# A hybrid decoder block: SBUF tiles of one size and one place, a weight chunk cut finer, a convolution's history kept apart

## The chip, the cores and the metric

The kernel runs on one core of one Trainium2 chip. A core has a matrix engine (PE; its weight loads are listed as PEld), a vector engine (DVE), an activation engine (ACT), a general engine (POOL), and a queue engine (SP) that issues every DMA of this kernel. The on-chip memory SBUF has 128 partitions; matmuls read their two operands from it and write to PSUM banks. The metric is the device time of one execution in microseconds (us), as a median over runs.

## What is computed

One decoder layer in float32 on a sequence of 2048 tokens and 1024 channels. Two groups of four heads (gated DeltaNet, and retention) share an input projection; their outputs are concatenated, projected and added to the input. Then follows a gated MLP with a causal convolution of width 3 over time between the up-projection and the activation.

```python
def _conv_glu_mlp(x, w_up, conv_w, w_down):
    hdn = jnp.einsum('bsd,df->bsf', x, w_up)
    hdn = _causal_dwconv(hdn, conv_w)
    g, u = jnp.split(hdn, 2, axis=-1)
    return jnp.einsum('bsf,fd->bsd', jax.nn.silu(g) * u, w_down)

def reference(x, ...):
    h = x
    for l in range(DEPTH):                      # DEPTH = 1
        n = _rms_norm(h, attn_norm_w[l])
        proj = jnp.einsum('bsd,dc->bsc', n, w_in[l])
        (gq, gk, gv, gg, ga, gb, rq, rk, rv, rg) = jnp.split(proj, split_idx, axis=-1)
        o_gdn = _gated_deltanet(gq, gk, gv, gg, ga, gb, ...)
        o_ret = _retention(rq, rk, rv, rg)
        mix = jnp.concatenate([o_gdn, o_ret], axis=-1)
        h = h + jnp.einsum('bsm,md->bsd', mix, w_out[l])
        n2 = _rms_norm(h, mlp_norm_w[l])
        h = h + _conv_glu_mlp(n2, w_up[l], mlp_conv_w[l], w_down[l])
    return _rms_norm(h, final_norm_w)
```

## The kernel before

**Precision.** Each operand of a large matmul is split into a rounded high part (an ACT copy) and a remainder (a DVE subtraction), stored as two halves of one tile. `mm3` (lines 91 to 97) multiplies high by high (line 95), high by low (96) and low by high (97), so that each product costs three matmuls.

**Three stages.** `mixers` (0 to 1364 us) makes the two head groups and the output projection, in four blocks of 512 tokens. `mlp_up` (1364 to 2306 us) makes the up-projection by a scheme of seven products (Strassen's), in two passes `q` over 22 groups of output channels; the convolution, the gating and the seven combinations for the next stage follow each group, and the combinations go to DRAM (`aud`). `mlp_down` (2330 to 2773 us) makes the down-projection in seven passes over eight token pairs.

**Tiles.** Every SBUF tile is made by `unit` with `U1` = 1056 floats (4,224 bytes) a partition, whatever it holds, so that any tile can take any other's place. A planner that runs at build time takes the count of buffers for each tag (the constants at the head and `BUFS`), gives each tile an address, puts the instructions of each engine in an order, and sets the waits. In the program before, tiles begin at 1,152 + 4,224 k bytes, k from 0 to 53; that is at 0, 128, 256 or 384 modulo 512.

**The order of the mixers.** `ORDER` names the items of a block in the order in which they are handed to the planner: `pro` (transposed input, its split `n1`, the row norms), `k0` (retention keys of the first head pair, and 8 extra columns `ab` from which `dec` makes the decays of the DeltaNet heads), `a0` to `a3` (a DeltaNet head: decay matrix `D`, keys and queries, values, and `gdn_base`, line 467 on, which writes the matrix `NA` to DRAM in transposed pieces, line 472, and solves a triangular system on POOL), `g0` to `g3` (its recurrence), `q`, `k`, `v`, `h` (retention), `G0` to `G3` (gates), `B0` to `B3` (output projection) and `Bn` (`n2`, line 711 on: the second norm, which scales four tiles `n2s` on DVE, line 724, and stores them). A name with a leading "-" stands for the same item of the block before. Weight chunks are loaded one item ahead (`LA` = 1).

**Weight chunks.** `load_chunk` (line 173 on) loads a chunk in pieces of `step` columns: in block 0 the raw weights (`wraw`, 2 buffers, line 185), which are split by ACT and DVE (187, 188) and stored split in DRAM (191); in later blocks the stored pieces (181). The chunk of `k0` has 264 columns for each of 8 row blocks; its pieces of 528 columns hold two row blocks each, in four tiles `wk`, and `wrow` finds row block k in tile k // 2.

**The convolution of the MLP.** `group` (line 832 on) collects the pre-activation of 1024 tokens in a tile `uc` of 2 + 1024 columns. In the second pass its first two columns are the last two of the first pass, kept in `mhalo` (line 873) and copied in by POOL (line 837). ACT makes tap 2 (867), DVE adds taps 1 and 0 (870), each over the shifted 1024 columns. `prep_x` (line 774 on) makes the split combinations of the input at the start of each pass, on POOL (786), ACT (767) and DVE (768).

Of the kernel before, what the change touches and what calls it, by code (L numbers as in the profile page):

```python
# [8 lines left out]
F32 = mybir.dt.float32  # L9
F32R = mybir.dt.float32r  # L10
AF = mybir.ActivationFunctionType
ALU = mybir.AluOpType
# [2 lines left out]

NW = 5
LA = 1
NHH = 3
NUU = 4
NVR = 5  # L20
NVV = 18
# [1 line left out]
NST = 4  # L23
NUC = 2
NACC = 6
NWU = 9
NWO = 5
NRAW = 2
BUFS = {"n1": 8, "ykq": 5, "kv": 6, "NA": 5, "TT": 2, "o": 4, "n2s": 4, "mT": 8, "xk": 2, "ca": 2, "h": 2,
        "mix": 4, "D": 4, "rk": 2, "rq": 2, "rv": 4, "Ar": 1, "Y": 2, "Nb": 2, "rot": 1, "rrow": 1}  # L30

ORDER = ("pro k0 dec a1 a0 q0 v0 h0 h1 a2 g1 q1 a3 g2 v1 G2 g0 k1 h2 g3 G0 h3 G1 G3 B0 B1 B2 B3 Bn")
P = 128
S = 2048
D = 1024
KT = D // P
TB = 512
# [4 lines left out]
NF = DFF // P  # L42
NP = NF // 2
# [3 lines left out]
ORD_DN = [1, 2, 6, 7, 5, 3, 4]  # L47


U1 = 1056  # L50


def unit(pool, tag, shape, dt=F32, **kw):

    n = int(np.prod(shape[1:]))
    t = pool.tile([P, U1], dt, tag=tag, name=tag, **kw)[:, :n]
    if len(shape) == 3:
        t = t.rearrange("p (a b) -> p a b", a=shape[1])
    elif len(shape) == 4:
        t = t.rearrange("p (a b c) -> p a b c", a=shape[1], b=shape[2])  # L60
    return t
# [3 lines left out]
def hybrid_block(ctx, tc, x, xT, w_kq, w_v, w_g, w_rk, w_r, w_o, w_u, w_d, cols, rows, fnr, masks, rot, out):  # L65
# [7 lines left out]
    NCOL = cols.shape[1]  # L73
    base = cp.tile([P, U1], F32, name="base")
    colt = base[:, :NCOL]
# [40 lines left out]
def mixers(ctx, tc, marks, drp, mm3, gamma, mhalf, n1w, n2w, gcw, gv127, epsr, n2d, hd,  # L116
           x, xT, w_kq, w_v, w_g, w_rk, w_r, w_o, rows, masks, rot):
    nc = tc.nc
    PE, ACT, DVE, POOL = nc.tensor, nc.scalar, nc.vector, nc.gpsimd
# [6 lines left out]

    pers, used = [], [U1]

    def pc(*shape):
        n = int(np.prod(shape))  # L130
        if used[0] + n > U1:
            pers.append(cp.tile([P, U1], F32, name=f"pers{len(pers)}"))
            used[0] = 0
# [33 lines left out]
        POOL.memset(t, 0.0)  # L167


    WQ = 528  # L170
    cache = {}

    def load_chunk(key, src):
        n = src.shape[1]
        step = WQ if n == 4 * WQ else 512
        qs = []
        for o in range(0, n, step):
            tg, nb = ("wco", NWO) if key[0] == "o" else ("wk", 4) if step == WQ else ("wc", NW)
            wc = unit(wp, tg, [P, 2, step], F32R, bufs=nb)
            if (key, o) in cache:  # L180
                nc.sync.dma_start(wc[:, :, :step].bitcast(F32), cache[key, o])
            else:
                if o % (2 * step) == 0:
                    raw2 = unit(wp, "wraw", [P, 2, step], bufs=NRAW)
                    nc.sync.dma_start(raw2.rearrange("p a n -> p (a n)"), src[:, o:o + 2 * step])
                raw = raw2[:, o // step % 2]
                ACT.activation(wc[:, 0], raw, AF.Copy)
                DVE.tensor_tensor(wc[:, 1], raw, wc[:, 0].bitcast(F32), op=ALU.subtract)  # L188
                nm = f"wd{len(cache)}"
                dt_ = cache[key, o] = drp.tile([P, 2, step], F32, name=nm, tag=nm, bufs=1)  # L190
                nc.sync.dma_start(dt_, wc[:, :, :step].bitcast(F32))
            qs.append(wc)
        return qs
# [4 lines left out]
        return t[:, 0, o:o + P], t[:, 1, o:o + P]  # L198

    def wrow(w, k, n):  # L200
        o = (k % 2) * n
        t = w[k // 2]
        return t[:, 0, o:o + n], t[:, 1, o:o + n]

    def al(tag, shape, dt=F32):
        return unit(ap_, tag, shape, dt, **({"bufs": BUFS[tag]} if tag in BUFS else {}))

# [37 lines left out]
    def A_items(b, st):  # L245
# [35 lines left out]
        def tokmajor(w, ncol, evac):  # L281
            n1 = st["n1"]
            for t in range(NT):
                ps = bank("tok")
                mm3(ps[:, :ncol],
                    [(n1[k][:, 0, t * P:(t + 1) * P], n1[k][:, 1, t * P:(t + 1) * P])
                     + wrow(w, k, ncol) for k in range(KT)])
                evac(t, ps)
# [445 lines left out]
    for b in range(NB + 1):  # L734
        for name in ORDER.split():
            c = b - 1 if name[0] == "-" else b
# [8 lines left out]
    for i, it in enumerate(seq):  # L745
        while nxt < len(order) and nxt <= done + la:
            loaded[order[nxt]] = load_chunk(*seq[order[nxt]][:2])
            nxt += 1
        if it[0] is not None:
            it[2](loaded.pop(i))  # L750
            done += 1
        else:
            it[2](None)
# [4 lines left out]
def mlp_up(ctx, tc, marks, drp, mm3, mcw, mhalo, n2d, wud, aud, w_u):  # L758
    nc = tc.nc
    PE, ACT, DVE, POOL = nc.tensor, nc.scalar, nc.vector, nc.gpsimd  # L760
    xp = ctx.enter_context(tc.tile_pool(name="xp", bufs=1))
    up = ctx.enter_context(tc.tile_pool(name="up", bufs=2))
    psu = ctx.enter_context(tc.tile_pool(name="psu", bufs=8, space=PSUM))
    T2 = 2 * TB
# [32 lines left out]
    def load_w(q, g):  # L797
        ws = {}

        def wtile(i):  # L800
            return unit(up, "wu", [P, 2, TB], F32R, bufs=NWU)
        if q == 1:
# [27 lines left out]
    def group(q, g, ws, xc, st):  # L830
        f0, kind = g // 2, g % 2
        us = []
        for j in range(2):
            u = unit(up, "uc", [P, 2 + T2], bufs=NUC)
            ci = kind * NF + f0 + j * NP
            if q:
                POOL.tensor_copy(u[:, :2], mhalo[:, ci])
            us.append(u)
        c11, c12 = us[0][:, 2:2 + TB], us[0][:, 2 + TB:]
        c21, c22 = us[1][:, 2:2 + TB], us[1][:, 2 + TB:]  # L840

        def prod(i, ps=None):
            first = ps is None
            if first:
                ps = psu.tile([P, TB], F32, tag="pp", name=f"p{i}")
            w = ws[i]
            mm3(ps, [(w[:, 0, kt * P:(kt + 1) * P], w[:, 1, kt * P:(kt + 1) * P], xc[i, kt][:, 0], xc[i, kt][:, 1])
                     for kt in range(4)], first=first, chk=not first)
            return ps
        add = lambda o, ps, a: DVE.tensor_tensor(o, ps, a, op=ALU.add)  # L850
        p1 = prod(1)
        ACT.activation(c12, p1, AF.Copy)
        prod(2, p1)
        ACT.activation(c11, p1, AF.Copy)
        add(c12, prod(6), c12)
        add(c21, prod(7), c12)
        p5 = prod(5)
        add(c22, p5, c21)
        add(c21, prod(4), c21)
        prod(3, p5)  # L860
        add(c12, p5, c12)
        accs = []
        for j in range(2):
            u = us[j]
            ci = kind * NF + f0 + j * NP
            acc = unit(up, "acc", [P, T2], bufs=NACC)
            ACT.activation(acc, u[:, 2:], AF.Copy, scale=mcw[:, ci, 2:3])  # L867
            for s in (1, 2):
                o = 0 if q else s
                DVE.scalar_tensor_tensor(acc[:, o:], u[:, 2 + o - s:2 - s + T2], mcw[:, ci, 2 - s:3 - s], acc[:, o:],  # L870
                                         op0=ALU.mult, op1=ALU.add)
            if q == 0:
                POOL.tensor_copy(mhalo[:, ci], u[:, T2:])
            accs.append(acc)
        if kind == 0:
            for a in accs:
                ACT.activation(a, a, AF.Silu)
            st["g"] = accs
            return
        for j in range(2):  # L880
            DVE.tensor_tensor(accs[j], st["g"][j], accs[j], op=ALU.mult)
        a11, a21 = accs[0][:, :TB], accs[0][:, TB:]
        a12, a22 = accs[1][:, :TB], accs[1][:, TB:]

        sts = [unit(up, "st", [P, 2, TB], bufs=NST) for j in range(2)]

        def comb(i, op, a, b_):
            t = sts[i // 2][:, i % 2]
            POOL.tensor_tensor(t, a, b_, op=op)
            return t  # L890
        s1 = comb(0, ALU.add, a21, a22)
        s2 = comb(1, ALU.subtract, s1, a11)
        s3 = comb(2, ALU.subtract, a11, a21)
        s4 = comb(3, ALU.subtract, a12, s2)
        for i, src in {1: a11, 2: a12, 4: a22, 5: s1, 6: s2, 7: s3, 3: s4}.items():
            marks["a", q, f0] = nc.sync.dma_start(aud[q, i][f0], src)
# [6 lines left out]
    for n, (q, g) in enumerate(gs):  # L903
        ws = nxt
        if n and g == 0:
            xc = prep_x(q)
        if n + 1 < len(gs):
            nxt = load_w(*gs[n + 1])
        group(q, g, ws, xc, st)
# [4 lines left out]
def mlp_down(ctx, tc, marks, mm3, sfa, mhalf, hd, aud, w_d, fnr, out):  # L914
# [77 lines left out]
    def addh(t, dh):  # L992
        h = unit(wq, "hh", [P, TB], bufs=NHH)
        nc.sync.dma_start(h, hd[t // NT][t % NT * P:(t % NT + 1) * P, dh * TB:(dh + 1) * TB])
        c = C[t][:, dh * TB:(dh + 1) * TB]
        DVE.tensor_tensor(c, c, h, op=ALU.add)
# [5 lines left out]
    for n, (i, tp) in enumerate(steps):  # L1002
# [17 lines left out]
        if i == 1:  # L1020
            ACT.activation(c12, ps, AF.Copy)
            h = unit(wq, "hh", [P, TB], bufs=NHH)
            nc.sync.dma_start(h, hd[t0 // NT][t0 % NT * P:(t0 % NT + 1) * P, :TB])
# [105 lines left out]
```

## Time and profile before

| what | value |
|---|---|
| median of 3 runs | 2778.41 us (2772.77 to 2778.88) |
| the profiled execution's own time | 2774.46 us |
| its span, first to last instruction | 2772.7 us |
| mean granted PE clock | 0.964 of full speed |
| PE busy | 2582.7 us, 93%, 14652 matmuls |
| DVE, ACT, POOL busy | 1496.9, 963.1, 976.4 us |
| DMA | 583.29 MB, 210 GB/s on average |

A matmul's listed duration (399 ns for 512 columns) runs past the start of the next one; what a matmul costs in a dense stretch is the distance between two starts, about 231 ns for 512 columns and 119 ns for 256. A busy share of 93% therefore says where PE had work, not how fast it went. Idle time of PE is what a change of order, of waits or of buffers can win back; the distance between starts is what a change of the operands' places could.

### The profile page before, as it was taken

Reading aid. Unit: us, or ns where it says so; the run is one execution under the profiler, and the core shown is the slowest. Engines: PE = TensorE matmul, PEld = TensorE weight load, DVE = VectorE, ACT = ScalarE, POOL = GpSimd, SP = SyncE. Lnnn points to the kernel's source line nnn. Section 1 sums busy time; section 2 is a strip of 40 time slices with the busy share of each in tenths; the row PEclk is TensorE's granted clock in tenths of the full one; section 3 lists DMA queues with packets and bytes.
Section 4 is the critical chain, followed back from the end, with each engine's and each line's share of the span. In section 5 each row is a group of like instructions: output and inputs, shape, how many; then the busy total and the mean of one; then the engine's idle time right before and its main releaser. Section 6 shows DMA issues by size and latency. Waiting matters only on the chain.

```text
span 2772.7 us, 40393 instructions
## 1 busy us (share of the span) xinstructions
PE 2582.7 (93%) x14652; PEld 2227.6 (80%) x14652; DVE 1496.9 (54%) x2795; ACT 963.1 (35%) x2086; POOL 976.4 (35%) x1638
## 2 busy tenths in 40 slices
PE   5999799999999999999679999979999996999998
PEld 5899798998889898898657777757888885888877
DVE  4655445434544525434387676766544544545685
ACT  4544343224422334322343344432222213433332
POOL 1655105540173404651153434344122220421161
PEclk8999799999999999998889999989999998999999
DMA  8657385436635455540557787785677765755693
GB/s 311 235 206 256 107 303 171 145 131 213 234 133 176 140 195 187 165 148 33 202 190 278 268 305 273 288 295 182 235 240 243 253 228 183 262 183 182 213 295 128
DMA packets 285384, 583.29 MB, mean 210 GB/s; under 512 B 39361, under 2 KB 136961, under 8 KB 285185
## 3 DMA queue, kind: packets, MB, share of 16 engines
q1 hardware_dynamic: 285184, 580.72, 60.2%
q8 instruction: 115, 1.88, 0.3%
q14 instruction: 85, 0.69, 0.1%
HBM read 390.21 MB, written 190.41 MB: 209 GB/s over the span
## 4 chain that ended last, share of the span: by engine, by line
PE 69%; DMA 8%; POOL 8%; DVE 7%; issue 5%; ACT 2%; SPq 1%; POOLq 0%; DVEq 0%; ACTq 0%
PE p L97 8%; PE p L96 8%; PE p L95 8%; PE d L97 5%; PE d L95 5%; PE d L96 5%; PE tok L95 4%; PE tok L97 4%; PE tok L96 4%; POOL pers L484 2%; PE wo L95 2%; POOL pers L482 2%; PE wo L96 2%; PE wo L97 2%; POOL st L816 1%
## 5 line engine op out<-in xcount | busy, mean ns | idle before, releaser
L95 PE MATMUL p<-x,wu 128*128 128x512 f32 x1232 | 486.5, 399 | 34.7 <-ACT x L767 30.0
L96 PE MATMUL p<-x,wu 128*128 128x512 f32 x1232 | 491.4, 399 | 25.9 <-DVE x L768 25.8
L97 PE MATMUL p<-x,wu 128*128 128x512 f32 x1232 | 482.5, 398 | 1.9 <-DVE wu L768 1.9
L95 PE MATMUL tok<-wc,n 128*128 128x256 f32 x1152 | 332.4, 290 | 9.1 <-DMA wc<-wd 7.3
L96 PE MATMUL tok<-wc,n 128*128 128x256 f32 x1152 | 330.6, 288 | 0.8 <-DVE wc L188 0.8
L97 PE MATMUL tok<-wc,n 128*128 128x256 f32 x1152 | 329.8, 287 | 0.0
L95 PEld LDWEIGHTS p<-x,wu 128*128 128x128 f32 x1232 | 234.1, 190 | 98.2 <-ACT x L767 33.2
L96 PEld LDWEIGHTS p<-x,wu 128*128 128x128 f32 x1232 | 234.2, 190 | 87.9 <-DVE x L768 35.7
L97 PEld LDWEIGHTS p<-x,wu 128*128 128x128 f32 x1232 | 234.5, 190 | 57.2 <-DVE wu L768 4.8
L850 DVE TENSOR_TENSOR uc<-p,uc 128x512 f32<-128x512 f32 x220 | 151.8, 690 | 232.4 <-PE p L97 218.2
L870 DVE SCALAR_TENSOR_TENSOR acc<-uc,base,acc 128x1024 f32<-128x1024 f32 (+2 forms) x176 | 215.3, 1279 | 34.6 <-ACT acc L867 34.4
L482 POOL TENSOR_TENSOR pers<-Nb,pers 128x124 f32<-128x124 f32 (+30 forms) x496 | 166.5, 336 | 189.2 <-DMA Nb<-z 154.0
L95 PEld LDWEIGHTS tok<-wc,n 128*128 128x128 f32 x1152 | 220.2, 192 | 11.3 <-DMA wc<-wd 8.0
L96 PEld LDWEIGHTS tok<-wc,n 128*128 128x128 f32 x1152 | 220.4, 191 | 2.0 <-DVE wc L188 1.2
L97 PEld LDWEIGHTS tok<-wc,n 128*128 128x128 f32 x1152 | 220.4, 192 | 0.3
L95 PE MATMUL d<-v,uu 128*128 128x512 f32 x448 | 177.6, 397 | 24.6 <-ACT uu L976 24.6
L484 POOL TENSOR_TENSOR pers<-pers 128x124 f32<-128x124 f32 (+30 forms) x496 | 171.6, 346 | 36.6
L97 PE MATMUL d<-v,uu 128*128 128x512 f32 x448 | 178.5, 398 | 2.1 <-DVE uu L977 2.1
L96 PE MATMUL d<-v,uu 128*128 128x512 f32 x448 | 177.4, 396 | 0.0
L95 PE MATMUL chm<-n,wc 128*128 128x512 f32 x384 | 154.7, 403 | 1.6 <-DMA wc<-wd 1.6
L96 PE MATMUL chm<-n,wc 128*128 128x512 f32 x384 | 153.5, 400 | 0.0
L97 PE MATMUL chm<-n,wc 128*128 128x512 f32 x384 | 153.2, 399 | 0.0
(243 smaller groups left out, 5424.0 us busy)
## 6 DMA issues: line engine op xcount, KB each, us to landing
wu<-wu SPq DMA_DIRECT2D x308, 512.0 KB, 5.6
wc<-wd SPq DMA_DIRECT2D x180, 512.0 KB, 5.1
wd<-wc SPq DMA_DIRECT2D x60, 512.0 KB, 6.1
ur<-au SPq DMA_DIRECT2D x56, 512.0 KB, 4.8
wco<-wd SPq DMA_DIRECT2D x48, 512.0 KB, 6.4
wur<-in_w_u SPq DMA_DIRECT2D x44, 512.0 KB, 6.3
au<-st SPq DMA_DIRECT2D x88, 256.0 KB, 2.5
vr<-in_w_d SPq DMA_DIRECT2D x44, 512.0 KB, 6.1
```

The source lines that it names most:

```text
L95: PE.matmul(ps, ah, bh, start=(first and i == 0), stop=False, skip_group_check=chk)
L96: PE.matmul(ps, ah, bl, start=False, stop=False, skip_group_check=chk)
L97: PE.matmul(ps, al, bh, start=False, stop=(i == n - 1), skip_group_check=chk)
L482: POOL.tensor_tensor(tm[:, :, :n], Nb[:, j:j + 1, j + 1:].to_broadcast([P, 4, n]), X[:, :, j:j + 1].to_broadcast([P, 4, n]), op=ALU.mult)
L484: POOL.tensor_tensor(X[:, :, j + 1:], X[:, :, j + 1:], tm[:, :, :n], op=ALU.add)
L816: POOL.tensor_tensor(t, a, b_, op=op)
L850: add = lambda o, ps, a: DVE.tensor_tensor(o, ps, a, op=ALU.add)
L870: DVE.scalar_tensor_tensor(acc[:, o:], u[:, 2 + o - s:2 - s + T2], mcw[:, ci, 2 - s:3 - s], acc[:, o:], op0=ALU.mult, op1=ALU.add)
```

## The change

All tiles get 1024 floats (4,096 bytes) a partition. A tensor `pad` of 56 floats, allocated ahead of all tiles, moves the first of them, so that tiles begin at 1,376 + 4,096 k bytes, which is 352 modulo 512 for each. Two kinds of tile were longer than 1024 floats, and are made differently:

- the chunk of `k0` is cut into eight pieces of 264 columns, one row block each, so that eight `wk` tiles, eight loads (in block 0 four raw loads, eight splits and eight stores) take the place of four;
- `uc` loses its two columns of history. Taps 1 and 0 run over the columns that have their predecessor in the tile, and in the second pass one or two columns at the front are added by a second, small DVE instruction that reads `mhalo`. The POOL copy of line 837 is gone.

With it go other counts of buffers, and another order of the mixers: `a0` and `q0` stand ahead of `a1`, `Bn` of a block is handed over after `q0` of the next block, `k1` stands ahead of `g0`, `g2` and `v1`, and the end of the block is `g3 h2 h3 G1 G0 G3 B0 B1 B2 B3`.

```diff
-NHH = 3
+NHH = 4
-NWU = 9
+NWU = 10
-BUFS = {"n1": 8, "ykq": 5, "kv": 6, "NA": 5, "TT": 2, "o": 4, "n2s": 4, "mT": 8, "xk": 2, "ca": 2, "h": 2,
-        "mix": 4, "D": 4, "rk": 2, "rq": 2, "rv": 4, "Ar": 1, "Y": 2, "Nb": 2, "rot": 1, "rrow": 1}
-
-ORDER = ("pro k0 dec a1 a0 q0 v0 h0 h1 a2 g1 q1 a3 g2 v1 G2 g0 k1 h2 g3 G0 h3 G1 G3 B0 B1 B2 B3 Bn")
+BUFS = {"n1": 8, "ykq": 5, "kv": 7, "NA": 5, "TT": 2, "o": 3, "n2s": 5, "mT": 8, "xk": 2, "ca": 2, "h": 2,
+        "mix": 4, "D": 6, "rk": 2, "rq": 2, "rv": 5, "Ar": 2, "Y": 4, "Nb": 3, "rot": 1, "rrow": 3}
+
+ORDER = ("pro k0 dec a0 q0 -Bn a1 v0 h0 h1 q1 a2 g1 a3 k1 g0 g2 v1 G2 g3 h2 h3 G1 G0 G3 B0 B1 B2 B3")
...
-U1 = 1056
+U1 = 1024
...
-    WQ = 528
+    WQ = 264
...
-        step = WQ if n == 4 * WQ else 512
+        step = WQ if n == KT * WQ else 512
...
-            tg, nb = ("wco", NWO) if key[0] == "o" else ("wk", 4) if step == WQ else ("wc", NW)
+            tg, nb = ("wco", NWO) if key[0] == "o" else ("wk", KT) if step == WQ else ("wc", NW)
...
     def wrow(w, k, n):
-        o = (k % 2) * n
-        t = w[k // 2]
+        kn = KT // len(w)
+        o = (k % kn) * n
+        t = w[k // kn]
...
-            u = unit(up, "uc", [P, 2 + T2], bufs=NUC)
-            ci = kind * NF + f0 + j * NP
-            if q:
-                POOL.tensor_copy(u[:, :2], mhalo[:, ci])
-            us.append(u)
-        c11, c12 = us[0][:, 2:2 + TB], us[0][:, 2 + TB:]
-        c21, c22 = us[1][:, 2:2 + TB], us[1][:, 2 + TB:]
+            us.append(unit(up, "uc", [P, T2], bufs=NUC))
+        c11, c12 = us[0][:, :TB], us[0][:, TB:]
+        c21, c22 = us[1][:, :TB], us[1][:, TB:]
...
-            ACT.activation(acc, u[:, 2:], AF.Copy, scale=mcw[:, ci, 2:3])
-            for s in (1, 2):
-                o = 0 if q else s
-                DVE.scalar_tensor_tensor(acc[:, o:], u[:, 2 + o - s:2 - s + T2], mcw[:, ci, 2 - s:3 - s], acc[:, o:],
-                                         op0=ALU.mult, op1=ALU.add)
+            ACT.activation(acc, u, AF.Copy, scale=mcw[:, ci, 2:3])
+            for t in (1, 2):
+                w = mcw[:, ci, 2 - t:3 - t]
+                DVE.scalar_tensor_tensor(acc[:, t:], u[:, :T2 - t], w, acc[:, t:], op0=ALU.mult, op1=ALU.add)
+                if q:
+                    DVE.scalar_tensor_tensor(acc[:, :t], mhalo[:, ci, 2 - t:], w, acc[:, :t],
+                                             op0=ALU.mult, op1=ALU.add)
             if q == 0:
-                POOL.tensor_copy(mhalo[:, ci], u[:, T2:])
+                POOL.tensor_copy(mhalo[:, ci], u[:, T2 - 2:])
...
+    nc.alloc_sbuf_tensor("pad", [P, 56], F32)
```

## The prediction

> **What bounds the kernel now.** I read the page's shares and its chain of waits first, then the busy time of each engine by stretches, then the waits of PE, and last the timelines around its stalls.
>
> ```profile
> PE 2582.7 (93%) x14652; PEld 2227.6 (80%) x14652; DVE 1496.9 (54%) x2795; ACT 963.1 (35%) x2086; POOL 976.4 (35%) x1638
> ...
> PE 69%; DMA 8%; POOL 8%; DVE 7%; issue 5%; ACT 2%; SPq 1%; POOLq 0%; DVEq 0%; ACTq 0%
> ```
>
> PE sets the time. Two things can change it: the distance between matmul starts, and PE's idle time, which the stretches locate (columns: window, its length, then busy time of PE, PEld, DVE, ACT, POOL, granted clock, DMA share, GB/s).
>
> ```profile
> 0.00:60.00 60.00, 30.69 (x162) 27.94 (x163) 23.79 (x67) 26.05 (x42) 8.27 (x29) 0.86 0.88 334
> 60.00:1290.00 1230.00, 1172.53 (x8412) 1088.02 (x8411) 579.90 (x1685) 448.90 (x1275) 495.66 (x1216) 0.97 0.52 180
> ...
> 1364.00:1410.00 46.00, 12.33 (x27) 6.55 (x25) 37.14 (x26) 16.18 (x28) 32.44 (x20) 0.56 0.73 263
> ...
> 1846.00:1890.00 44.00, 22.28 (x61) 14.28 (x61) 36.79 (x30) 18.05 (x29) 33.31 (x21) 0.67 0.68 244
> 1890.00:2306.00 416.00, 416.00 (x1799) 338.13 (x1797) 205.27 (x219) 94.49 (x110) 91.67 (x85) 1.00 0.65 224
> 2306.00:2330.50 24.50, 0.04 (x1) 0.00 (x0) 10.68 (x11) 5.70 (x8) 4.96 (x4) 0.54 0.54 175
> ```
>
> PE idles 29.3 us at the head, 57.5 us spread over the mixers, 33.7 us where the MLP begins, 21.7 us where its second pass begins, 24.5 us before the down-projection, and nothing in the second pass itself, where only matmul distance counts.
>
> **Part 1, the tiles' places.** No view shows addresses, but the order of PE's instructions in the trace and the addresses in the program before can be put side by side. For each 512-column matmul I took the distance to the next start (those under 260 ns, 6,400 of 6,696), sorted by where its moving operand begins relative to the weights that are loaded meanwhile for the next matmul, modulo 512 bytes:
>
> ```
> difference   0: 1680 matmuls, mean 230.92 ns
> difference 128: 1531 matmuls, mean 231.86 ns
> difference 256: 1561 matmuls, mean 231.15 ns
> difference 384: 1628 matmuls, mean 231.61 ns
> all           : mean 231.38 ns
> ```
>
> With all tiles at one place and all slices at multiples of 512 bytes inside them, every such pair has difference 0 after the change: 0.46 ns x 6,696 = **-3.1 us**. At 256 columns the same table gives 118.66 ns for difference 0 and for all: nothing. Sorted by the operand's own start modulo 512, the 512-column means lie between 231.1 and 231.6. Vector, activation and POOL instructions of one form, and the landing times of DMAs, sorted by their tile's start, show no trend either (taps of 1024 columns 1279 to 1284 ns at each of the places). So this part is worth -3.1 us by these rows. Before, all tiles begin at multiples of 128; 352 is not one. The only moving operands off that grid are slices of `wk` (line 95 to 97, 264 columns): 121.47 ns on the 64-byte grid (162 matmuls), 122.09 ns off it (174). That 0.6 ns is the other bound: for 12,072 split matmuls +7.2 us. I take -3.1, because the two `wk` groups are small and their spread (118 to 127 ns) is ten times the difference.
>
> [...]
>
> **Part 2, history apart.** Removed: 44 POOL copies (line 837). Added: 22 groups x 2 tiles x 2 taps = 88 small DVE instructions. The nearest row, the mixers' like instruction over 1 to 3 columns (line 241), has a median of 218 ns, so 19.2 us of DVE in the second pass. PE is busy 416.00 of 416.00 us there and DVE 205.27, so PE hides them; without this cover they would cost those 19.2 us. In the last group nothing covers them: acc L870, acc L881, POOL's combinations, the store and the load back run one after another while PE waits. Four of them: **+0.9 us**.
>
> The copies held POOL's queue. Here is POOL where the second pass begins, then PE:
>
> ```profile
> 1849.32 0.18 POOL L873 COPY base<-uc 128x2 f32<-128x2 f32 x1 [6.18 <-DVE uc L850]
> 1854.36 5.28 POOL L837 COPY uc<-base 128x2 f32<-128x2 f32 x2 [4.85 <-DVE acc L870]
> 1859.60 2.94 POOL L889 TENSOR_TENSOR st<-acc 128x512 f32<-128x512 f32 x2
> 1862.50 2.98 POOL L786 TENSOR_TENSOR st<-acc 128x512 f32<-128x512 f32 x2
> ...
> 1869.53 0.79 PE L95 MATMUL p<-x,wu 128*128 128x512 f32 x1 [6.84 <-ACT x L767]
> ```
>
> Two copies of two columns waited 4.85 us for `uc` to come free and then took 5.28 us; behind them in POOL's queue stood line 889, and line 786, whose result the stalled matmul waits for through ACT. DVE ends the first product that line 889 reads (L881, 1855.31 for 1.22 us) at 1856.5, so the combinations can begin 3.1 us earlier than 1859.60. I take **-3.0 us** (0 if the loads of `acc` become the wait, at most -5.3). The other waits of line 837, 288.4 us in all, cost PE nothing.
>
> **Part 3, the norm of the block before.** DVE at the start of block 1:
>
> ```profile
> 388.91 0.28 DVE L596 TENSOR_TENSOR rk<-tok,rot 128x128 f32<-128x128 f32 x1
> 389.69 4.63 DVE L724 TENSOR_TENSOR n2s<-n2s,rrow 128x1024 f32<-128x1024 f32 x4 [0.50 <-ACT rrow L721]
> 394.24 0.22 DVE L588 TENSOR_SCALAR pers<-tok,pers 128x8 f32<-128x8 f32 x1
> ...
> 395.78 0.23 DVE L588 TENSOR_SCALAR pers<-tok,pers 128x8 f32<-128x8 f32 x1 [0.53 <-PE tok L97]
> ```
>
> The four scalings of `Bn` stand between the evacuations of `k0`, which came every 2.94 us (385.24, 388.18) and so could have been at 391.1 and 394.1. The last is 1.7 us late, and with it the decays, `D`, `NA`, and the store of `NA` that SP's queue waits for, with weight loads behind it (SP's issues, then PE):
>
> ```profile
> 420.36 1.60 SPq L181 DMA_DIRECT2D wc<-wd  x2
> 430.38 0.80 SPq L472 DMA_DIRECT2D z<-NA  x2
> ...
> 436.17 1.01 SPq L181 DMA_DIRECT2D wc<-wd  x2
> ...
> 441.38 0.58 PE L95 MATMUL tok<-wc,n 128*128 128x256 f32 x1 [3.67 <-DMA wc<-wd]
> ```
>
> PE lists 7.3 us in two such waits. With `Bn` after `q0` I take 1.7 us from each: **-3.4 us** (bounds 0, if the wait moves to the chunk of `a1`, and -7.3). Late next are the n2 stores, which only the MLP reads.
>
> **Part 4, the finer chunk.** Six more issues on SP in block 0 (two raw loads, four stores) at 0.32 to 0.42 us: 2.2 us. PE's first matmul (9.82 us) and its second stretch (8.54 us idle) wait for `n`, whose loads share that queue. Half-size first pieces put 0.53 MB less ahead of them, 1.6 us at the head's 334 GB/s; the third piece must wait for one of two `wraw` buffers, at worst one landing, 5.7 us in the chain of waits. Between -1.6 and +5.7 I take **+1.0 us**, nearest to the issues less the saving. Four more reloads in each later block (1.3 us of SP) are issued hundreds of us ahead (`wk` loads from 45.2 us on) and cost nothing unless that lead goes.
>
> **Part 5, buffers and the rest of the order.** The tenth `wu` tile: PE lists 4.9 us of waits for `wu`, but ACT's waits there are for the raw weights (68.1 us) and POOL (61.4), none for a free tile: **-0.5** (0 to -4.9). A fourth `hh` tile: nothing waits for it. The rest of the order leaves the same six chunk items after `a3` as cover for the last solves; I take 0, between a gain of all 57.5 us of the mixers' idle time and the loss in the third rival.
>
> **Sum.** -3.1 + 0.9 - 3.0 - 3.4 + 1.0 - 0.5 = -8.1 us. The profiled execution took 2774.5 us: 2766.4. It lies 3.9 us under the median and 1.7 under the mean of all four executions shown (2776.1), so I put the sum on that mean: **2768 us**. About 0.2% (5.6 us) is what a measurement of this kernel can tell from no change.
>
> **Rivals.** *The order fills the gaps.* The new order could close a third of the mixers' 57.5 us, 19.2, of which 3.4 are counted: 2768 - 15.8 = 2752. For it: bare recurrences cost PE over 26 us (sps, wps, ks). Against: DVE sits between those matmuls in any order.
>
> *Slower: the eight `wk` tiles.* The shorter tile gives 55 slots instead of 54, but `wk` holds eight for four, from long before its use: three fewer for all else. Counting tiles between first write and last read, all 54 are in use around 260 to 320, 520 to 620 and 850 to 960 us. If a load then waits for a slot, three tiles come one landing (5.1 us, wc) later at each of the three block ends, and `Bn`'s tiles, held longer, take back part 3: 15.3 + 3.4 = 18.7, 2787 us. It decides once PE waits more than some 15 us for wc. Against: no wait for a slot costs PE now.
>
> *Off the grid.* If 0.6 ns is real, 7.2 instead of -3.1: 2778 us. [...]
>
> *The planner undoes it.* It orders each queue by its own estimate, so `Bn` and POOL's combinations may land where they were: only the places count, 2773 us.
>
> **How the numbers follow.** Forecast 0.45 (own range 2758 to 2776: 0.38 faster, 0.06 within, 0.01 slower), order 0.17 (faster), slots 0.20 (slower), grid 0.10 (half within, half slower), planner 0.08 (0.06 within, 0.02 slower). Together faster 0.55, same 0.17, slower 0.28. The range from 2750 to 2790 leaves out about half of the second and two fifths of the third case.
>
> **What would show it.** Distances of 512-column starts near 230.9 ns (above 232: the grid); POOL's line 786 following line 881 at once where the second pass begins, and PE's stall there 3 us shorter; evacuations of `k0` 2.9 us apart in all blocks; the wait of PE for wc under 7.3 us; PE still fully busy in the second pass. I am wrong if the mixers' idle time moves by more than 10 us either way.

## The result, and the profile after

The change made the kernel slower by half a per cent: 2788.65 us (median of 20 runs, 2774.93 to 2796.57) against 2773.69 (20 runs, 2769.09 to 2783.85), a ratio of **1.0048, 95% interval 1.0036 to 1.0059** (the quotient of the two medians alone would be 1.0054). The prediction was 2768, faster. The profiled execution took 2785.95 us, with a span of 2784.2 against 2772.7.

The page of the changed kernel, busy time and chain, answers to the first two lines shown of before:

```profile
PE 2576.7 (93%) x14652; PEld 2244.0 (81%) x14652; DVE 1501.6 (54%) x2887; ACT 964.2 (35%) x2090; POOL 932.3 (33%) x1594
...
PE 53%; DMA 12%; POOL 12%; issue 11%; DVE 9%; ACT 3%; SPq 1%; POOLq 0%; DVEq 0%; ACTq 0%
```

PE is busy 6 us less, yet the span is 11.5 us longer; in the chain of waits its share falls from 69% to 53%, and issue (5% to 11%), DMA, POOL and DVE take most of the difference. So PE got faster and waits more. Both can be seen. First, a stretch of the second up pass in which PE is never idle, in before, after and the first experiment (columns: window, length, busy time of PE, PEld, DVE, ACT, POOL with counts, granted clock, DMA share, GB/s):

```profile
2000.00:2300.00 300.00, 300.00 (x1301) 244.04 (x1300) 149.36 (x159) 68.85 (x79) 68.34 (x64) 1.00 0.67 229
```

```profile
2000.00:2300.00 300.00, 300.00 (x1325) 248.51 (x1324) 157.32 (x224) 70.12 (x81) 44.20 (x35) 1.00 0.76 245
```

```profile
2000.00:2300.00 300.00, 300.00 (x1293) 242.58 (x1292) 154.19 (x220) 69.55 (x80) 40.74 (x32) 1.00 0.74 238
```

The 300 us hold 1,301 matmuls of 512 columns before (230.6 ns each), 1,325 after (226.4), and 1,293 in e1_places_undone, which has the instructions of the changed kernel but tiles at many places (232.0).

Second, the waits of PE, of before and then of after (columns: waiting tile and line, releaser, us in total, times, longest):

```profile
PE sps L553 <- DVE pers L551: 10.2, 21, 1.1
PE wps L549 <- DVE kv L545: 9.7, 19, 1.3
PE tok L95 <- DMA wc<-wd: 7.3, 2, 3.7
...
PE p L95 <- ACT wu L767: 3.0, 4, 1.3
...
PE ro L637 <- DVE pers L640: 1.1, 6, 0.3
...
PE mxt L310 <- DVE mix L308: 0.3, 1, 0.3
```

```profile
PE wps L550 <- DVE kv L546: 14.7, 27, 2.7
PE sps L554 <- DVE pers L552: 14.2, 29, 0.9
...
PE p L95 <- ACT wu L768: 8.9, 10, 1.7
PE tok L95 <- DMA wc<-wd: 8.3, 11, 1.5
PE ro L637 <- DVE Ar L631: 6.3, 1, 6.3
...
PE mxt L311 <- DVE mix L309: 3.8, 3, 2.2
```

The recurrences (`wps`, `sps`), retention (`ro`) and the output mix (`mxt`) wait longer: PE's queue reaches them before DVE has made their operands. In the MLP, the waits for `wu` grow from 3.0 to 8.9 us. A few waits shrink: `ks` goes from 6.2 to 3.1 us between 60 and 1400 us, and `kqtr` from 8.0 to 2.3.

To put both on one scale, I took for every matmul of a trace the distance to the next start and subtracted a base of my choice, one for all traces: for a split matmul (lines 95 to 97) of 512 columns 227.0 ns, the mean of the changed kernel; of 256 columns 116.5 and of 264 columns 119.9, about the shortest tenth before; for all others 112, near their median before (111). An excess under 40 ns counts as **distance**; one of about the length of the matmul, where the clock record stands at half for most of it, as **half clock**; the rest as **gaps**. The sums by stage, in us, each before -> after:

```
stage             distance         half clock      gaps
mixers block 0    -4.6 ->  -3.9    12.0 -> 14.2    71.2 -> 79.1
mixers block 1    -5.6 ->  -6.3     0.5 ->  2.4    33.1 -> 39.3
mixers block 2    -5.4 ->  -6.4     1.5 ->  3.5    33.6 -> 35.8
mixers block 3    -5.4 ->  -4.4     7.6 ->  8.4    52.4 -> 55.5
up, first pass     8.2 ->   0.1     3.6 ->  3.2    45.7 -> 50.1
up, second pass    7.1 ->  -0.5     4.2 ->  7.3    44.1 -> 44.5
down               8.4 ->  -0.5     2.9 ->  3.5     3.6 ->  6.7
sum                2.7 -> -21.8    32.3 -> 42.4   283.7 -> 310.8
```

The places win 24.5 us, all of it in the MLP; 27.1 us of new gaps, 19.4 of them in the mixers, and 10.1 us at half clock take it back: +12.7. The first matmul starts 1.0 us earlier, which leaves 11.7, close to the 11.5 us between the spans.

### The profile page after: what moved, and what is told of

Read it like the earlier page. It is cut to its first block, busy times and chain, and to the rows that moved or that the text cites. A ratio compares the mean times of both kernels' runs of the same rounds, so it can differ in the third digit from the quotient of the medians.

```text
span 2784.2 us, 40486 instructions
## 1 busy us (share of the span) xinstructions
PE 2576.7 (93%) x14652; PEld 2244.0 (81%) x14652; DVE 1501.6 (54%) x2887; ACT 964.2 (35%) x2090; POOL 932.3 (33%) x1594
## 4 chain that ended last, share of the span: by engine, by line
PE 53%; DMA 12%; POOL 12%; issue 11%; DVE 9%; ACT 3%; SPq 1%; POOLq 0%; DVEq 0%; ACTq 0%
PE p L96 5%; PE p L95 5%; PE p L97 5%; PE d L97 5%; PE d L95 5%; PE d L96 4%; POOL st L817 3%; POOL pers L485 3%; POOL pers L483 3%; DMA wur<-in_w_u 3%; PE tok L95 3%; PE tok L97 3%; PE tok L96 3%; PE wo L95 2%; DVE x L769 2%
## 5 line engine op out<-in xcount | busy, mean ns | idle before, releaser
L867 DVE SCALAR_TENSOR_TENSOR acc<-uc,base,acc 128x1022 f32<-128x1022 f32 (+1 forms) x176 | 220.5, 1278 | 33.9 <-ACT acc L864 33.8
L95 PEld LDWEIGHTS tok<-wc,n 128*128 128x128 f32 x1152 | 222.7, 194 | 18.3 <-issue 7.0
L96 PEld LDWEIGHTS tok<-wc,n 128*128 128x128 f32 x1152 | 223.4, 194 | 3.5 <-DVE wc L188 2.6
L97 PEld LDWEIGHTS tok<-wc,n 128*128 128x128 f32 x1152 | 222.0, 194 | 0.5
L888 POOL TENSOR_TENSOR st<-acc 128x512 f32<-128x512 f32 x44 | 57.8, 1336 | 479.8 <-DVE acc L880 479.8
L97 PE MATMUL chm<-n,wc 128*128 128x512 f32 x384 | 152.0, 396 | 1.5 <-DVE wc L188 1.5
L95 PE MATMUL chm<-n,wc 128*128 128x512 f32 x384 | 152.2, 396 | 0.0
```

The source lines that it names most:

```text
L95: PE.matmul(ps, ah, bh, start=(first and i == 0), stop=False, skip_group_check=chk)
L96: PE.matmul(ps, ah, bl, start=False, stop=False, skip_group_check=chk)
L97: PE.matmul(ps, al, bh, start=False, stop=(i == n - 1), skip_group_check=chk)
L867: DVE.scalar_tensor_tensor(acc[:, t:], u[:, :T2 - t], w, acc[:, t:], op0=ALU.mult, op1=ALU.add)
```

## The experiments

Each ran in several rounds beside the kernel before. The three sums of the same kind (us), each from one profiled execution, with the ratio to before, from all runs. One execution can lie some us off its median: that of e3 took 2790.60 us (median 2784.41), that of e8 2752.05 (median 2757.67).

```
kernel                        distance  half clock   gaps   ratio
before                            2.7      32.3     283.7   1
after                           -21.8      42.4     310.8   1.0048
e1_places_undone                  4.4      33.7     311.5   1.0122
e2_place_0                      -22.0      39.5     313.9   1.0049
e3_old_order                    -20.3      44.5     311.5   1.0031
e4_new_order_on_before            5.8      49.4     312.6   1.0174
e5_history_alone                  3.7      27.5     284.5   1.0000
e6_counts_alone                   3.9      34.8     292.6   1.0022
e7_four_wk_tiles                -18.0      55.9     320.8   1.0126
e8_old_order_one_tile_less      -20.7      24.1     294.3   0.9936
e9_bn_moved_alone                 0.3      25.6     303.1   1.0033
e10_rest_of_order                 3.6      56.5     314.2   1.0193
e11_head_of_order                 6.7      40.3     304.3   1.0109
e12_tail_of_order                 5.3      46.5     321.3   1.0169
```

The first column falls by 21 to 25 us wherever all tiles share one place, and nowhere else. The others change most where the order does.

**e1_places_undone.** In the changed kernel, tiles of 4,128 bytes, which begin at 16 places modulo 512; the order of every engine stays as it was.

```diff
-U1 = 1024
+U1 = 1032
```

> The kernel after with 1032 floats a tile instead of 1024, so that its 55 tiles begin at 352 + 32 k modulo 512, all places mixed; every engine's instructions and their order are those of the kernel after. Theory (one place speeds the 512-column matmuls and slows the 256-column ones a little, and something else in the change loses more): 512-column starts go back from 226.8 to about 231.4 ns, 256-column starts from 120.0 to about 118.7, so 6,696 x 4.6 - 4,992 x 1.3 = 24 us more than after: ratio to before about 1.013. Rival (the shorter distance comes with the other order of instructions, and places do nothing): distances stay at 226.8 and 120.0, ratio 1.005 as after.

Measured: 2807.61 us (2803.65 to 2810.84), ratio 1.0122 (1.0102 to 1.0142). Against the changed kernel that is +0.7%, some 20 us; its distance sum is 26.2 us higher, its half-clock sum 8.7 lower. One place modulo 512 is worth this. It is the one gain of the change, and smaller than the gaps and the half clock that come with the rest (37.2 us).

**e2_place_0.** In the changed kernel, tiles at 0 instead of 352 modulo 512.

```diff
-    nc.alloc_sbuf_tensor("pad", [P, 56], F32)
+    nc.alloc_sbuf_tensor("pad", [P, 96], F32)
```

> The kernel after with a pad of 96 floats, so that all tiles begin at 0 modulo 512 instead of 352; instructions and order unchanged. Theory (only the distance between the places of two operands counts, which is 0 modulo 512 either way): 226.8 and 120.0 ns, ratio 1.005. Rival (352 itself counts): 512-column starts at 230 ns or more and a ratio of 1.012 or more.

Measured: 2786.17 us, ratio 1.0049 (1.0029 to 1.0070), the same as the changed kernel. It counts that all tiles share one place; which of these two it is doesn't. With it the rival "off the grid" falls.

**e3_old_order.** The geometry of the changed kernel and its separate history, with the counts and the order string of before. The chunk of `k0` keeps four tiles, of 4,608 bytes (nine times 512), and its raw pieces are loaded one by one.

```diff
-    t = pool.tile([P, U1], dt, tag=tag, name=tag, **kw)[:, :n]
+    t = pool.tile([P, 1152 if tag == "wk" else U1], dt, tag=tag, name=tag, **kw)[:, :n]
...
-    WQ = 264
+    WQ = 528
```

> The kernel after with the order and all counts of buffers of before. To make room, the chunk of 264 columns is held in four tiles of 4,608 bytes (a multiple of 512, all still at 352 modulo 512) with raw pieces of 528 columns. Theory (the order and the counts, which the eight wk tiles forced, lose some 38 us, and the places win 24): blocks of the mixers take about as long as before (372, 323, 324, 332 us), 512-column starts 226.8 ns, total about 2750 us, ratio 0.991. Rival (the history kept apart, or something in the tiles' size, loses it): ratio 1.003 or more.

Measured: 2784.41 us, ratio 1.0031 (1.0015 to 1.0046); a miss, where 0.991 was expected. The places gave 23.0 us, but gaps and half clock took 40.0. An old order string isn't the old order: the planner puts PE's instructions in a sequence of its own, and it differed from that of before at 361 of 13,654 places (counted by the kinds of tile that an instruction names), most of them in the second half of blocks 1 and 2. e8 below takes this up.

**e4_new_order_on_before.** The kernel before, with the order string and all counts of the changed one.

> The kernel before, tiles of 4,224 bytes at mixed places, chunk in four tiles and history in the tile, with the order and all counts of buffers of after. Theory (order and counts lose by themselves): blocks of the mixers some 20 to 26 us longer in sum than before, ratio about 1.008 to 1.013. Rival (they lose only with the eight wk tiles holding slots): ratio 0.998 to 1.002.

Measured: 2823.66 us, ratio 1.0174 (1.0150 to 1.0198). Order and counts, without any other part of the change, lose more than the change as a whole does.

**e5_history_alone, e6_counts_alone, e7_four_wk_tiles.** The kernel before with the two `group` hunks of the diff (e5); with `NHH`, `NWU` and `BUFS` of the diff (e6); the changed kernel with four `wk` tiles made as in e3 (e7).

> The kernel before with the conv history apart alone (tiles of 4,224 bytes, chunk, order and counts as before). PE's order is that of before up to the last part of the second up pass. Theory 'order' (the loss of the change comes from what stands where in PE's queue in the mixers): the mixers stay as they were (PE's idle time there within 5 us of before), the 88 small DVE instructions lie behind PE, and the ratio is between 0.997 and 1.002. Rival 'history' (the runs with the history apart all wait longer in the MLP: 11 us in the changed kernel, 18 us in the one with the old order): the MLP's waits grow by 8 us or more and the ratio is 1.003 or higher. The prediction's own part 2 says -2.1 us, 0.9992.

> The kernel before with the new buffer counts alone (all counts of the changed kernel, order string as before). PE's order differs from before at 68 of 13,654 places. Theory 'order': the 47 us that order and counts lost together came from the order string, so this one is between 0.998 and 1.003. Rival 'counts' (more buffers let loads and solves run earlier and collide, whatever the order): 1.008 or higher.

> The changed kernel with the 264-column chunk taken back: four wk tiles (of 4,608 bytes, so that all tiles still begin at 352 modulo 512) in place of eight, raw pieces of 528 columns. Theory 'order': the order string stays the new one, so the gaps stay: ratio to before 1.003 to 1.010. Rival 'slots' (the prediction's third rival: eight wk tiles hold slots): the gaps of the mixers fall by 15 us or more and the ratio is 1.000 or lower.

Measured: e5 2775.83 us, **1.0000 (0.9985 to 1.0015)**; e6 2781.29, **1.0022 (1.0006 to 1.0037)**; e7 2812.45, **1.0126 (1.0108 to 1.0145)**. The history shows neither a cost nor a gain; the interval leaves room for some 4 us either way. The counts cost little. Four `wk` tiles instead of eight make the changed kernel 0.8% slower, where the slots rival expected a gain. Whether the pieces themselves have a price can't be read from that: PE's sequence moved at 1,131 places with them, and gaps (+10.0) and half clock (+13.5) grew.

**e8_old_order_one_tile_less.** e3_old_order with 4,096 bytes less memory. This changes no instruction and no place modulo 512, only the planner's choices; PE's sequence differs from that of before at 206 places, none in those halves of blocks 1 and 2.

```diff
-    nc.alloc_sbuf_tensor("pad", [P, 56], F32)
+    nc.alloc_sbuf_tensor("pad", [P, 1080], F32)
```

> The kernel of e3_old_order (all tiles at one place modulo 512, old order string and counts, history apart, chunk in four wk tiles) with 4,096 bytes less memory, so that its planner has one tile less at hand. PE's order now differs from that of before at 206 places, none of them between the 3,200th and 3,600th or the 5,200th and 5,600th instruction, where e3_old_order differed in 246. Theory 'order' (e3_old_order lost what the places gave because projections had moved away from the waits of the solves in blocks 1 and 2): in these two blocks PE's gaps and half-clock time together fall by 15 us or more against e3_old_order, the 512-column distance stays near 227 ns, and the ratio to before is 0.993 to 0.999. Rival 'speed for waits' (a faster TensorE only waits longer for the other engines, whatever the order): the gaps stay, ratio 1.001 to 1.004.

Measured: **2757.67 us (2752.05 to 2765.62), ratio 0.9936 (0.9915 to 0.9958)**, faster than both kernels. In blocks 1 and 2 gaps and half clock fell from 90.0 us in e3 to 74.0 (before 68.7). That is 16.0 of the 38.5 us between these two executions; 26.7 us lie between their medians, and how much of those belongs to the two blocks isn't known. Block 1 from its first matmul to that of block 2, in before, e3 and e8 (columns as above):

```profile
381.80:704.30 322.50, 309.93 (x2280) 288.35 (x2279) 145.77 (x444) 112.82 (x328) 123.29 (x308) 0.99 0.53 182
```

```profile
378.10:717.40 339.30, 320.20 (x2280) 298.02 (x2279) 145.10 (x444) 113.44 (x328) 122.38 (x308) 0.96 0.51 173
```

```profile
371.30:698.40 327.10, 312.07 (x2280) 289.69 (x2278) 145.94 (x444) 112.77 (x328) 123.30 (x308) 0.99 0.53 177
```

The same 2,280 matmuls take 322.5, 339.3 and 327.1 us. Where e3 loses, PE's timeline (start, duration, instruction, and idle time before it with its releaser) reads:

```profile
632.21 0.49 PE L554 MATMUL wps<-kv,TT 128*128 128x128 f32 x2 [0.45 <-DVE kv L550]
633.14 0.49 PE L558 MATMUL sps<-pers,kv 128*128 128x128 f32 x2 [0.45 <-DVE pers L556]
...
634.36 0.61 PE L644 MATMUL rr<-rv,rk 128*128 128x128 f32 x4
638.37 0.80 PE L642 MATMUL ro<-pers,ykq 128*128 128x128 f32 x2 [3.40 <-DVE pers L645]
638.96 0.64 PE L641 MATMUL ro<-rv,Ar 128*128 128x128 f32 x2
...
643.65 0.58 PE L549 MATMUL ks<-pers,ykq 128*128 128x128 f32 x2
...
644.90 0.36 PE L95 MATMUL wo<-wco,mT 128*128 128x256 f32 x1
645.10 0.28 PE L96 MATMUL wo<-wco,mT 128*128 128x256 f32 x1
```

DVE's timeline in e3 at the same time:

```profile
634.83 1.41 DVE L283 SCALAR_TENSOR_TENSOR n<-xk,base,n 128x512 fp32r<-128x512 f32 x2 [1.74 <-ACT n L282]
636.16 0.34 DVE L559 SCALAR_TENSOR_TENSOR pers<-pers,pers,sps 128x128 f32<-128x128 f32 x1
...
637.37 0.75 DVE L283 SCALAR_TENSOR_TENSOR n<-xk,base,n 128x512 fp32r<-128x512 f32 x1 [0.66 <-ACT n L282]
638.03 0.28 DVE L645 SCALAR_TENSOR_TENSOR pers<-pers,rr 128x128 f32<-128x128 f32 x1
```

And PE's timeline in e8, at the same step of the recurrence:

```profile
618.56 0.49 PE L554 MATMUL wps<-kv,TT 128*128 128x128 f32 x2 [0.44 <-DVE kv L550]
618.80 0.36 PE L95 MATMUL tok<-wc,n 128*128 128x256 f32 x1
...
621.64 0.28 PE L97 MATMUL tok<-wc,n 128*128 128x256 f32 x1
621.76 0.39 PE L558 MATMUL sps<-pers,kv 128*128 128x128 f32 x2
...
622.88 0.61 PE L644 MATMUL rr<-rv,rk 128*128 128x128 f32 x4
623.71 0.49 PE L642 MATMUL ro<-pers,ykq 128*128 128x128 f32 x2 [0.22 <-DVE pers L645]
```

DVE's timeline in e8:

```profile
620.26 2.08 DVE L283 SCALAR_TENSOR_TENSOR n<-xk,base,n 128x512 fp32r<-128x512 f32 x3 [0.82 <-ACT n L282]
622.25 0.34 DVE L559 SCALAR_TENSOR_TENSOR pers<-pers,pers,sps 128x128 f32<-128x128 f32 x1
...
623.38 0.28 DVE L645 SCALAR_TENSOR_TENSOR pers<-pers,rr 128x128 f32<-128x128 f32 x1
```

In e8, 24 projections (618.80 to 621.76) stand between `wps` and `sps`, and DVE works through its queue meanwhile: the norm of the next block's input (line 283), which waits for ACT, and the step of the recurrence behind it. In e3 these projections were already used up. `wps` and `sps` follow each other bare, DVE stands 1.74 us and then 0.66 us at line 283 for ACT with lines 559 and 645 queued behind it, and PE waits 3.40 us for line 645. The clock record stands at 0.5 from 637.2 to 644.1, and from the end of that wait to 644.1 every matmul takes about 1.5 to 2 times as long: from `ro` at 638.96 to the next start it is 0.43 us, from `ro` at 633.69 it was 0.23. The wait costs more than its own length.

**e9 to e12, the order string in parts.** All on the kernel of e6, with one part of the new string each, in this turn: `-Bn` after `q0` (e9), all but that (e10), and of e10's part the first half up to `a3` (e11) or the second from `a3` on (e12).

```diff
-ORDER = ("pro k0 dec a1 a0 q0 v0 h0 h1 a2 g1 q1 a3 g2 v1 G2 g0 k1 h2 g3 G0 h3 G1 G3 B0 B1 B2 B3 Bn")
+ORDER = ("pro k0 dec a1 a0 q0 -Bn v0 h0 h1 a2 g1 q1 a3 g2 v1 G2 g0 k1 h2 g3 G0 h3 G1 G3 B0 B1 B2 B3")
...
+ORDER = ("pro k0 dec a0 q0 a1 v0 h0 h1 q1 a2 g1 a3 k1 g0 g2 v1 G2 g3 h2 h3 G1 G0 G3 B0 B1 B2 B3 Bn")
...
+ORDER = ("pro k0 dec a0 q0 a1 v0 h0 h1 q1 a2 g1 a3 g2 v1 G2 g0 k1 h2 g3 G0 h3 G1 G3 B0 B1 B2 B3 Bn")
...
+ORDER = ("pro k0 dec a1 a0 q0 v0 h0 h1 a2 g1 q1 a3 k1 g0 g2 v1 G2 g3 h2 h3 G1 G0 G3 B0 B1 B2 B3 Bn")
```

> The kernel of e6_counts_alone (before with the new buffer counts, 1.0022) with one step of the order string changed: Bn, the norm of the block before, after q0 instead of at the block's end. The prediction's part 3: the evacuations of k0 are freed and 3.4 us saved, ratio to before 1.001. Rival: with Bn gone from the block's head the planner puts PE's projections at 1,297 other places, and the solves are left bare: 1.005 or higher.

> The kernel of e6_counts_alone (1.0022) with the new order string, but Bn left at the block's end. If the rest of the order bears the loss of 1.5% that the whole string made on before (1.0174 against 1.0022), the ratio is 1.010 to 1.018 and PE's waits of the solves (sps, wps, ks, mxt) are longer by 10 us or more. If Bn bears it, 1.005 or lower. The prediction took the rest of the order for nothing.

> The kernel of e6_counts_alone (1.0022) with only the first half of the new order string, up to a3 (a0 q0 a1 v0 h0 h1 q1 a2 g1 a3), the rest and Bn as before. e10_rest_of_order lost 1.7% against e6_counts_alone. Theory 'head': the solves and recurrences wait because the heads' projections are made in another turn (q1 ahead of a2 and g1): ratio 1.011 to 1.020. Rival 'tail': 1.005 or lower.

> The kernel of e6_counts_alone (1.0022) with only the second half of the new order string, from a3 on (a3 k1 g0 g2 v1 G2 g3 h2 h3 G1 G0 G3). Theory 'tail': k1 and the gates are used up ahead of the last recurrences, which then stand bare: 1.011 to 1.020. Rival 'head': 1.005 or lower. The prediction's sentence that the same six chunk items after a3 remain as cover says 1.002, that of e6_counts_alone.

Measured: e9 2784.57 us, 1.0033 (1.0017 to 1.0048); e10 2830.05, **1.0193 (1.0172 to 1.0214)**; e11 2806.44, 1.0109 (1.0088 to 1.0131); e12 2826.51, 1.0169 (1.0140 to 1.0198). Moving `Bn` is worth nothing that the intervals can tell from e6's 1.0022. The rest of the string loses 1.7% against e6, and both its halves lose, 0.9% and 1.5%, together more than the whole: each theory of the last two runs expected one half to be free, and neither is. PE's waits in e10, between 60 and 1400 us, show the kind:

```profile
PE sps L553 <- DVE pers L551: 18.2, 33, 1.4
PE wps L549 <- DVE kv L545: 12.9, 23, 2.8
PE ro L637 <- DVE pers L640: 9.5, 4, 3.5
PE mxt L310 <- DVE mix L308: 7.3, 4, 2.2
PE ro L636 <- DVE Ar L630: 6.9, 1, 6.9
```

These come to 54.8 us in 65 waits; before, `sps`, `wps`, `ro` and `mxt` had 21.3 in the same window. It is many short waits, with one of 6.9 us among them, not a single stall.

## Why the prediction was wrong, step by step

**The step that failed is in Part 5: "The rest of the order leaves the same six chunk items after `a3` as cover for the last solves; I take 0".** Counting items of the string was no measure of cover. What counts is which projections still stand in PE's queue at each single wait: the timelines of e3 and e8 show it at one wait, and for the 65 waits of e10 it is inferred. By e10 this term was some +48 us on the kernel before (1.0193 against e6's 1.0022). In the changed kernel it was smaller: gaps and half clock grew by 37.2 us in all, some of it in the MLP, which the string doesn't order. Of these 37.2 us 10.1 are at half clock, for which the sum had no term.

The prediction's own sign of being wrong was the mixers' idle time moving by more than 10 us. By its measure, PE's listed idle time, the matmuls that stood between 60 and 1290 us went only from 57.5 to 64.9 us, and all four blocks from 83.3 to 93.9; the gaps, by distances between starts, grew by 19.4. A matmul's listed duration runs past the start of the next one (399 ns before for 512 columns, where starts are about 231 apart), so listed idle time hides the first part of every wait, and the sign was too weak for many short ones.

**Part 1, the places: the direction held, but the size was -24.5 us, not -3.1, and pairs were the wrong unit.** The table of the prediction sorted matmuls by one pair, the moving operand and the next weights. The trace of before held more. Sort its 512-column matmuls by how many matmuls in a row, up to this one, had both operands at one and the same place, with at least the next one there too (the last of a run is in no row):

```
length of the run     512 columns: matmuls, mean ns    256 columns
not in one                4713   231.5                   3495   118.7
1 to 3                     897   231.3                    677   118.5
4 or 5                     136   228.9                     52   118.7
6 or more                   64   227.3                     30   120.0
```

The last row is close to what the whole kernel shows after the change: 227.0 ns for 512 columns (-4.4), and 119.6 for 256, slightly longer. Before, a pair at one place saved little (230.9 ns against 231.4 for all), and a run of six or more nearly all (227.3). The trace of the changed kernel has the same ramp at the head of its runs: 231.9 ns for the first three matmuls of 512 columns in a run (109 of them), 230.2 for the fourth and fifth (88), 226.9 from the sixth on. With tiles scattered over four places only 64 of 6,404 matmuls were in such a run, so the pair table could not see it. e1 and e2 have the same loads, and their matmuls of 512 columns differ by 5.6 ns: 1,293 in the 300 us from 2000 to 2300 in e1 (232.0 ns each), 1,325 in e2 (226.4). What in SBUF or PE makes the difference was not tried.

**Part 2, the history: no gain that the runs can tell from nothing, where -2.1 was expected.** The interval of e5, some 4 us either way, would hold -2.1 too; its working did not hold. The copies went, but POOL did not start 3.1 us earlier. Timelines of the changed kernel where the second pass begins, of POOL, then DVE, then PE:

```profile
1878.28 4.47 POOL L888 TENSOR_TENSOR st<-acc 128x512 f32<-128x512 f32 x2 [8.30 <-DVE acc L880]
1882.71 2.49 POOL L787 TENSOR_TENSOR st<-acc 128x512 f32<-128x512 f32 x2
```

```profile
1875.78 2.35 DVE L880 TENSOR_TENSOR acc<-acc 128x1024 f32<-128x1024 f32 x2
1878.05 1.89 DVE L769 TENSOR_TENSOR x<-acc,x 128x512 fp32r<-128x512 f32 x3
```

```profile
1889.26 1.22 PE L95 MATMUL p<-x,wu 128*128 128x512 f32 x2 [6.37 <-ACT x L768]
```

POOL now waits for the second of DVE's products too (line 880), and its two combinations, started while DVE runs line 769, take 4.47 us, where they took 2.94 before. PE's stall went from 6.84 to 6.37 us: -0.5 of the -3.0. The 88 small DVE instructions did hide: from 2000 to 2300 us of the changed kernel PE is busy 300.00 us of 300.

**Part 3, `Bn`: no gain, where -3.4 was expected.** The evacuations of `k0` (line 588 before, 589 after) did come more evenly, though not 2.9 us apart throughout. DVE's timeline in the changed kernel, at the head of block 1:

```profile
394.98 0.23 DVE L589 TENSOR_SCALAR pers<-tok,pers 128x8 f32<-128x8 f32 x1 [1.92 <-PE tok L97]
...
397.89 0.23 DVE L589 TENSOR_SCALAR pers<-tok,pers 128x8 f32<-128x8 f32 x1 [1.89 <-PE tok L97]
...
401.70 0.23 DVE L589 TENSOR_SCALAR pers<-tok,pers 128x8 f32<-128x8 f32 x1 [2.79 <-PE tok L97]
...
404.58 0.23 DVE L589 TENSOR_SCALAR pers<-tok,pers 128x8 f32<-128x8 f32 x1 [1.86 <-PE tok L97]
```

The longest interval is 3.8 us instead of 6.1. But PE's wait for `wc` became 11 waits of 8.3 us instead of two of 7.3. The link from the decays to that wait did not hold.

**Part 4, the finer chunk:** PE's first matmul starts at 8.81 us, 1.0 earlier, not 1.0 later; small, with the sign wrong. What its longer wait in the row norms takes (`rrp`, 15.3 us for 10.9) its gaps in front of `wk` give back (7.9 us for 11.9).

**Part 5, the tenth `wu` tile:** no gain either, where -0.5 was expected. PE's waits for ACT's `wu` are 9.9 us in e6, which has the tenth tile and the old places, and 3.0 before.

**The rivals.** "The eight `wk` tiles" gave 2787 us, close to the median, but not for its reason, so the match is luck: it asked for over 15 us of waits for `wc`, which were 8.3, and with four tiles (e7, in another sequence) the kernel is slower still. "Off the grid" fell with e2. "The order fills the gaps" named the right place, with the wrong sign.

**Why e8 wins.** It keeps 23.4 us of the places, its gaps grow by 10.6, and its half clock falls by 8.2: -21.0, and -1.1 at the head, against 22.4 us between the spans of the two profiled executions (18.7 between the medians). Of the gaps, 8.8 are in the MLP, where PE waits longer for `x`, `wu` and `uu`; that a faster PE is the reason is likely, but not shown. Some of the rest is luck of the order: in block 0, where its sequence differs at over 130 places, gaps and half clock fall by 9.0 us.

What stays open: which single move of the string bares which wait, since both halves lose, and whether the finer chunk has a value of its own, as it couldn't be parted from the sequence.

## What to carry to other kernels

If the matrix engine is never idle for hundreds of us, as here in the second up pass (416.00 of 416.00 us busy before), the operands' places in SBUF are worth a look (they gave 24.5 us here): sort the distances in the trace by runs of matmuls with equal places, not by pairs. If a planner orders the queues, a change of tile size, of counts or of memory is a change of order too: compare the sequences first, and then time one version that has the new geometry with the old sequence. A wait of a few us can cost more than itself: behind the one of 3.40 us in e3 matmuls took about 1.5 to 2 times as long for another 5.7 us.

## What the hardware showed that I had not expected

Tiles at one place modulo 512 bytes made 512-column matmuls 2% faster (231.4 to 227.0 ns) and 256-column ones 1% slower (118.7 to 119.6). The place itself did not matter at 0 and 352 (1,325 matmuls in the same 300 us with either), and tiles that agree modulo 128 only had almost none of it (before, 231.4 ns, against 232.2 for the 16 places of e1). Tiles that agree modulo 256 only were not tried.

The clock record moves in steps of 3.41 us: its intervals are whole multiples of that, all 35 that end within the trace of before and all 41 of the changed kernel. Half clock came without a long wait, too. In the changed kernel the record stands at full speed from 543.48 to 546.89 us, with PE busy for 2.21 of these 3.41 us and no listed wait above 0.44 us. From 546.89 to 557.13 it stands at half, and split matmuls of 256 columns start 0.21 us apart there instead of 0.12. In e3 the record fell at 637.2, when the wait of 3.40 us had lasted 2.3, and it stood at 0.5 again from 657.7 to 664.5, after a stretch whose listed waits were at most 0.71 us each. What the falls share is how little PE worked in the step just before. Taken step by step, the 14 traces have 297 falls: none came after a step with PE busy for more than 75% of it, and no step with PE busy for less than 43% was followed by full clock. In between, both happened. In before and after, the 37 falls came after steps with PE busy for 0 to 65%.
